# Linear attention on one core: V loaded whole and spread on chip, last two groups stored over the SP queue

## The chip, the core and the metric

The kernel runs on one core of a Trainium2 chip. A core has a matrix engine (TensorE, "PE" in the profile; its weight loads are listed apart as "PEld"), a vector engine (VectorE, "DVE"), a scalar engine (ScalarE, "ACT"), GpSimd ("POOL") and SyncE ("SP"), each with its own stream of instructions, and 16 DMA engines that move data between the large memory (HBM, "dram" in the names) and the memory on the core (SBUF). Results of the matrix engine land in a third memory, PSUM. An engine runs its instructions in order and waits on semaphores for the others. In this kernel DMAs are issued from two places: POOL's queue and SP's queue.

The metric is the device time of one execution in microseconds (us); lower is better. The kernel before took 129.44 us, the median of 8 runs (128.91 to 130.25).

## The reference

Q, K and V have 8 batches, 12 heads, 512 rows and 64 columns, in 4-byte floats. There is no softmax: a feature map replaces it, so the keys and values of a head shrink to one 64x64 matrix.

```python
Q_feat = np.maximum(0, Q) + 1
K_feat = np.maximum(0, K) + 1
KV = np.einsum('bhkd,bhkv->bhdv', K_feat, V)
K_sum = np.sum(K_feat, axis=2)
numerator = np.einsum('bhqd,bhdv->bhqv', Q_feat, KV)
denominator = np.einsum('bhqd,bhd->bhq', Q_feat, K_sum)
return numerator / (denominator[:, :, :, None] + 1e-10)
```

There is little arithmetic for each byte: three inputs and one output of 12.58 MB each have to pass between HBM and the core.

## The kernel before

The 96 heads are worked in 12 groups of 8 heads. A group's K, V and Q are each 1.05 MB in HBM. They are viewed as two blocks of 128 partitions with 16 rows of 64 columns on every partition, so one head of a block lies on 32 partitions. POOL's DMAs turn 4-byte floats into bf16 as they move them; K of group 0 alone comes over SP unchanged, as 4-byte floats.

One matmul serves four heads of a block at once, although they share the partitions, because V is laid out in blocks: the buffer `v_blk` has five column blocks; block b (0 to 3) holds V on the 32 partitions of head b and zeros elsewhere, so that each head's sum stays in its own columns. The fifth block, the edge, holds a one for each head in its first four columns and gives the key sums (`K_sum`). There are three such buffers (`NV = 3`), zeroed once at the start, partly by VectorE and partly by ScalarE; later loads overwrite only the parts that hold V. To place V in its blocks, `load_v` issues four DMAs per group, one for each 32 partitions.

The stages of a group are these.

- `k_features` and `q_features`: VectorE, two instructions each, L116; max(x + 1, 1) into the tiles `kf` and `qf`.
- `keys_values`: 32 matmuls, L141, into PSUM; ScalarE copies the result into `kva_diag`, L151 and L152.
- `transposes`: 16 transposes of Q features on the matrix engine, L160, and two copies by ScalarE into `qt`, L161.
- `output`: 32 matmuls, L173, in four parts; VectorE takes the reciprocal of the denominators, L183, and multiplies, L184, from PSUM into the output tile `o_sb`.
- `store`: one DMA of 1.05 MB from POOL, L107; for the last group two halves from SP, L110.

The order is written out by hand. In step g the kernel issues the K, Q features of g, the transposes of g-1, the output of g-2, keys_values of g, then on POOL's queue the loads of K, V and Q of g+3 (`AHEAD`) and the store of g-3 (`LAG`). K and Q have four input buffers each (`IN_BUFS`), the output has six (`OUT_BUFS`). A load waits until its buffer is free: for V that is when keys_values of three groups before is done. Every DMA of POOL also waits for the one issued eight places before it on that queue, since they share a semaphore. After the loop the last group is finished, and groups 8 to 11 are stored.

Of the kernel before, what the change touches and what calls it, by code (L numbers as in the profile page):

```python
# [8 lines left out]
FP32 = mybir.dt.float32  # L9
BF16 = mybir.dt.bfloat16  # L10
ALU = mybir.AluOpType

BANK = 512
IN_BUFS = 4
OUT_BUFS = 6
LAG = 3
AHEAD = 3


@with_exitstack  # L20
def kernel(
# [4 lines left out]
    V: bass.AP,  # L26
    out: bass.AP,
):

# [5 lines left out]
    nc = tc.nc  # L37

    B, H, S, D = Q.shape
    P = 128  # L40
    C = 8
    C2 = 2 * C
    NPAIR = B * H * S // (P * C)
    NP = 4
    NG = NPAIR // NP
# [3 lines left out]
    def view(t, c):  # L49
        return t.flatten_outer_dims().rearrange("(n p c) d -> p n c d", p=P, c=c)  # L50

    q_dram = view(Q, C2)
    k_dram = view(K, C2)
    v_dram = view(V, C2)
    o_dram = view(out, C)

    const = ctx.enter_context(tc.tile_pool(name="const", bufs=1))
    head_pool = ctx.enter_context(tc.tile_pool(name="head_pool", bufs=1))
    in_pool = ctx.enter_context(tc.tile_pool(name="in_pool", bufs=IN_BUFS))
    feat_pool = ctx.enter_context(tc.tile_pool(name="feat", bufs=2))  # L60
# [6 lines left out]

    identity = const.tile([P, P], BF16, name="identity")
    NV = 3
    v_blk = [const.tile([P, 5, 2, C2, D], BF16, name=f"v_blk{i}") for i in range(NV)]  # L70
    ones = const.tile([P, 4], BF16, name="ones")
    zero = const.tile([P, 1], FP32, name="zero")
    kva_diag = [const.tile([P, 4, 2, D1], BF16, name=f"kva_diag{i}") for i in range(NV)]

    k_in = {}
    q_in = {}
    kfs = {}
    qfs = {}
    qts = {}
    outs = {}  # L80

    def load_k(g):
        k_raw = (head_pool if g == 0 else in_pool).tile(
            [P, 2, C2, D], FP32 if g == 0 else BF16, name="k_raw"
        )
        (nc.sync if g == 0 else nc.gpsimd).dma_start(  # L86
            out=k_raw, in_=k_dram[:, g * 2 : g * 2 + 2]
        )
        k_in[g] = k_raw

    def load_v(g):
        for b in range(4):
            nc.gpsimd.dma_start(  # L93
                out=v_blk[g % NV][32 * b : 32 * b + 32, b],
                in_=v_dram[32 * b : 32 * b + 32, 2 * g : 2 * g + 2],
            )

    def load_q(g):
        q_raw = in_pool.tile([P, 2, C2, D], BF16, name="q_raw")
        nc.gpsimd.dma_start(out=q_raw, in_=q_dram[:, g * 2 : g * 2 + 2])  # L100
        q_in[g] = q_raw

    def store(g):
        o_sb = outs.pop(g)
        o_to = o_dram[:, g * NP : g * NP + NP]
        if g < NG - 1:
            nc.gpsimd.dma_start(out=o_to, in_=o_sb)  # L107
            return
        for h in range(2):
            nc.sync.dma_start(out=o_to[:, h:NP:2], in_=o_sb[:, h:NP:2])  # L110

    def edge(i):
        return v_blk[i][:, 4, :, :, 0:4].rearrange("p n c j -> p (n c) j")

    def feature(dst, src):
        nc.vector.tensor_scalar(  # L116
            out=dst, in0=src, scalar1=1.0, scalar2=1.0, op0=ALU.add, op1=ALU.max
        )

    def k_features(g):  # L120
        k_raw = k_in.pop(g)
        kf = feat_pool.tile([P, C2, 2, D], BF16, name="kf")
        for n in range(2):
            feature(kf[:, :, n], k_raw[:, n])
        kfs[g] = kf

    def q_features(g):
        q_raw = q_in.pop(g)
        qf = feat_pool.tile([P, C2, 2, D], BF16, name="qf")
        for half in range(2):  # L130
            cs = slice(half * C, half * C + C)
            feature(qf[:, cs].rearrange("p c n d -> p n c d"), q_raw[:, :, cs])
        qfs[g] = qf

    def keys_values(g):
        kf = kfs.pop(g)
        vb = v_blk[g % NV]
        kva_ps = psum_kva.tile([P, 5, D], FP32, name="kva_ps")
        for c in range(C2):
            for n in range(2):  # L140
                nc.tensor.matmul(  # L141
                    kva_ps[64 * n : 64 * n + 64],
                    lhsT=kf[:, c, n, :],
                    rhs=vb[:, :, n, c, :],
                    start=(c == 0),
                    stop=(c == C2 - 1),
                )
        kva = kva_diag[g % NV]
        for n in range(2):
            ps = slice(64 * n, 64 * n + 64)  # L150
            nc.scalar.copy(out=kva[ps, :, n, 0:D], in_=kva_ps[ps, 0:4, :])  # L151
            nc.scalar.copy(out=kva[ps, :, n, D], in_=kva_ps[ps, 4, 0:4])  # L152

    def transposes(g):
        qf = qfs.pop(g)
        qt = mid_pool.tile([P, C, P, 2], BF16, name="qt")
        for half in range(2):
            qt_ps = psum_qt.tile([P, C, P], BF16, name="qt_ps")
            for c in range(C):
                nc.tensor.transpose(qt_ps[:, c, :], qf[:, half * C + c, :, :], identity)  # L160
            nc.scalar.copy(out=qt[:, :, :, half], in_=qt_ps)  # L161
        qts[g] = qt

    def output(g):
# [26 lines left out]
                )  # L191
        outs[g] = o_sb

    with tc.manual_schedule():
        nc.gpsimd.memset(zero, 0.0)
        load_k(0)
        load_q(0)
        load_k(1)
        load_q(1)
        nc.vector.memset(ones, 0.0)  # L200
        for b in range(4):
            nc.vector.memset(ones[32 * b : 32 * b + 32, b : b + 1], 1.0)  # L202
        flat = [t.rearrange("p b n c d -> p (b n c d)").bitcast(FP32) for t in v_blk]
        width = flat[0].shape[1]
        part = width * 4 // 7
        nc.vector.memset(flat[0][:, 0:part], 0.0)  # L206
        nc.scalar.copy(  # L207
            out=flat[0][:, part:width], in_=zero.to_broadcast([P, width - part])
        )
        nc.vector.tensor_copy(out=edge(0), in_=ones[:, None, :].to_broadcast([P, 2 * C2, 4]))  # L210
        load_v(0)
        nc.vector.memset(flat[1][:, 0:part], 0.0)  # L212
        nc.scalar.copy(
            out=flat[1][:, part:width], in_=zero.to_broadcast([P, width - part])
        )
        nc.vector.tensor_copy(out=edge(1), in_=ones[:, None, :].to_broadcast([P, 2 * C2, 4]))
        make_identity(nc, identity)
        for t in kva_diag:
            nc.gpsimd.memset(t, 0.0)  # L219
        load_v(1)  # L220
        load_k(2)
        k_features(0)
        q_features(0)
        nc.vector.memset(flat[2][:, 0:part], 0.0)  # L224
        nc.scalar.copy(
            out=flat[2][:, part:width], in_=zero.to_broadcast([P, width - part])
        )
        nc.vector.tensor_copy(out=edge(2), in_=ones[:, None, :].to_broadcast([P, 2 * C2, 4]))
        load_v(2)
        load_q(2)  # L230
        for g in range(NG - 1):
            if g:
                k_features(g)
                q_features(g)
                transposes(g - 1)
            if g >= 2:
                output(g - 2)
            keys_values(g)
            if g + AHEAD < NG:
                load_k(g + AHEAD)  # L240
                load_v(g + AHEAD)
                load_q(g + AHEAD)
            if g >= LAG:
                store(g - LAG)
        last = NG - 1
        k_features(last)
        transposes(last - 1)
        output(last - 2)
        q_features(last)
        keys_values(last)  # L250
        transposes(last)
        output(last - 1)
        output(last)
        for g in range(last - LAG, NG):
            store(g)
# [30 lines left out]
```

## Time and profile before

One execution was recorded by the hardware profiler. It took 129.44 us, of which 127.7 lie between its first and its last instruction (the span).

| what | value |
|---|---|
| median of 8 runs | 129.44 us |
| the profiled execution, own time | 129.44 us |
| its span | 127.7 us |
| PE busy | 68.2 us (53%) |
| VectorE busy | 66.1 us (52%) |
| ScalarE busy | 47.2 us (37%) |
| POOL busy | 54.0 us (42%) |
| POOL's DMA queue | 29.89 MB in 13088 packets |
| SP's DMA queue | 2.10 MB in 816 packets |
| V's loads, L93 | 48 issues, mean 549 ns on POOL, median 9.4 us from issue to landing |
| K's and Q's loads from POOL | 11 and 12 issues, 712 and 731 ns, 12.0 and 11.2 us to landing |
| stores from POOL, L107 | 11 issues, 772 ns, 12.0 us to landing |

The page also divides the span into 40 slices of 3.2 us and gives for each the busy share of the engines in tenths and the bytes moved; the bytes are counted as they are written. Stretches of any length can be asked for in the same way. A group of instructions is a row: line, engine, operation, written and read names with shapes, count, busy time, mean duration in ns, and the idle time before it. The chain of waits follows the execution back from its last event to what released it, step by step.

### The profile page before, as it was taken

To read this page: it belongs to the slowest core of one execution; us is meant where nothing else is said; L and a number is where in the kernel's file an instruction comes from. 1 tells how busy PE (TensorE), PEld (TensorE's weight loads), DVE (VectorE), ACT (ScalarE), POOL (GpSimd) and SP (SyncE) were. 2 spreads that over 40 slices of the span, in tenths; PEclk is the share of its full clock that TensorE was granted. 3 is DMA by queue.
4 is the path that set the end of the run, shared out by engine and by line. 5 is a ranking of instruction groups with operands and counts; after the bars stand their busy time and mean duration, and the time that the engine had idled before them with its cause. 6 is when DMAs were issued, how large, how long until landed. Compare 5 with 4: busy or idle time off the path is not lost.

```text
span 127.7 us, 2373 instructions
## 1 busy us (share of the span) xinstructions
PE 68.2 (53%) x960; PEld 50.7 (40%) x960; DVE 66.1 (52%) x155; ACT 47.2 (37%) x76; POOL 54.0 (42%) x92
## 2 busy tenths in 40 slices
PE   0000099939569494895804932951970896853000
PEld 0000077626446373674603721741750675632000
DVE  4898702095292775929309408606524739498000
ACT  7940006950911809045540090081063045640000
POOL 6695775517345274543543462372274240201000
PEclk9999999976985999599997798699599599996555
DMA  3999999999999999999999999999999999999980
GB/s 81 336 212 209 207 207 209 209 210 210 210 205 214 207 211 211 208 341 243 209 307 278 195 264 323 208 235 351 205 220 360 213 211 375 418 415 418 404 318 1
DMA packets 13914, 32.13 MB, mean 252 GB/s; under 512 B 1360, under 2 KB 1360, under 8 KB 13904
## 3 DMA queue, kind: packets, MB, share of 16 engines
q0 software_dynamic: 13088, 29.89, 99.6%
q1 hardware_dynamic: 816, 2.10, 4.5%
q8 instruction: 7, 0.11, 0.3%
q14 instruction: 3, 0.02, 0.0%
HBM read 37.75 MB, written 12.58 MB: 394 GB/s over the span
## 4 chain that ended last, share of the span: by engine, by line
DMA 69%; DVE 11%; issue 4%; POOL 4%; PE 4%; POOLq 0%; DVEq 0%
DMA v_blk<-in_V_dram 24%; DMA out_dram<-o_sb 18%; DMA q_raw<-in_Q_dram 18%; DMA k_raw<-in_K_dram 9%; DVE o_sb L184 6%; POOL v_blk L93 4%; PE kva_ps L141 4%; DVE v_blk L206 2%; DVE recip L183 1%; DVE qf L116 1%; DVE kf L116 1%; DVE ones L202 0%; POOL q_raw L100 0%; DVE ones L200 0%; POOLq L107 0%
## 5 line engine op out<-in xcount | busy, mean ns | idle before, releaser
L141 PE MATMUL kva_ps<-v_blk,kf 128*64 128x320 bf16 x384 | 38.0, 367 | 15.7 <-DMA v_blk<-in_V_dram 15.7
L173 PE MATMUL o_ps<-kva_diag,qt 128*64 128x130 bf16 x384 | 20.6, 247 | 32.8 <-DVE o_sb L184 32.3
L93 POOL DMA_DIRECT2D v_blk<-in_V_dram x48 | 26.2, 549 | 27.8 <-DMA k_raw<-in_K_dram 12.9
L141 PEld LDWEIGHTS <-kf 128*64 128x64 bf16 x384 | 26.6, 138 | 23.7 <-DVE qf L116 15.7
L184 DVE TENSOR_TENSOR o_sb<-o_ps,recip 128x512 f32<-128x512 f32 x48 | 33.2, 691 | 1.6
L151 ACT CAST kva_diag<-kva_ps 64x256 bf16<-64x256 f32 x24 | 8.9, 371 | 64.8 <-PE kva_ps L141 64.4
L161 ACT COPY qt<-qt_ps 128x1024 bf16<-128x1024 bf16 x24 | 29.5, 1300 | 0.3
L173 PEld LDWEIGHTS <-qt 128*64 128x64 bf16 x384 | 13.7, 121 | 38.6 <-DVE o_sb L184 36.8
L116 DVE TENSOR_SCALAR qf<-q_raw 128x1024 bf16<-128x1024 bf16 x24 | 9.2, 426 | 33.1 <-DMA q_raw<-in_Q_dram 33.1
L107 POOL DMA_DIRECT2D out_dram<-o_sb x11 | 8.5, 772 | 19.9 <-DMA q_raw<-in_Q_dram 7.0
L116 DVE TENSOR_SCALAR kf<-k_raw 128x1024 bf16<-128x1024 bf16 (+1 forms) x24 | 10.9, 495 | 10.5 <-DMA k_raw<-in_K_dram 10.5
L160 PE MATMUL qt_ps<-identity,qf 128*128 128x128 bf16 x192 | 13.1, 223 | 0.0
L160 PEld LDWEIGHTS <-qf 128*128 128x128 bf16 x192 | 11.1, 100 | 3.5 <-issue 3.2
L86 POOL DMA_DIRECT2D k_raw<-in_K_dram x11 | 7.8, 712 | 8.8 <-DMA out_dram<-o_sb 5.6
L183 DVE RECIPROCAL recip<-o_ps 128x8 f32<-128x8 f32 x48 | 9.5, 198 | 3.6 <-PE o_ps L173 3.6
L100 POOL DMA_DIRECT2D q_raw<-in_Q_dram x12 | 8.8, 731 | 4.2 <-DMA v_blk<-in_V_dram 2.4
L152 ACT CAST kva_diag<-kva_ps 64x4 bf16<-64x4 f32 x24 | 4.0, 168 | 0.0
L206 DVE MEMSET v_blk<- 128x2925 f32 x1 | 2.5, 2496 | 0.7 <-DVE ones L202 0.7
L224 DVE MEMSET v_blk<- 128x2925 f32 x1 | 2.5, 2496 | 0.6 <-issue 0.6
L212 DVE MEMSET v_blk<- 128x2925 f32 x1 | 2.5, 2496 | 0.6 <-issue 0.6
L219 POOL MEMSET kva_diag<- 128x520 bf16 x3 | 2.0, 719 | 0.0
L207 ACT COPY v_blk<-zero 128x2195 f32<-128x2195 f32 x1 | 2.0, 2019 | 0.0
(15 smaller groups left out, 7.9 us busy)
## 6 DMA issues: line engine op xcount, KB each, us to landing
out_dram<-o_sb POOLq DMA_DIRECT2D x11, 1024.0 KB, 12.0
q_raw<-in_Q_dram POOLq DMA_DIRECT2D x12, 512.0 KB, 11.2
v_blk<-in_V_dram POOLq DMA_DIRECT2D x48, 128.0 KB, 9.4
k_raw<-in_K_dram POOLq DMA_DIRECT2D x11, 512.0 KB, 12.0
k_raw<-in_K_dram SPq DMA_DIRECT2D x1, 1024.0 KB, 4.9
out_dram<-o_sb SPq DMA_DIRECT2D x2, 512.0 KB, 7.5
```

The source lines that it names most:

```text
L86: (nc.sync if g == 0 else nc.gpsimd).dma_start(out=k_raw, in_=k_dram[:, g * 2 : g * 2 + 2])
L93: nc.gpsimd.dma_start(out=v_blk[g % NV][32 * b : 32 * b + 32, b], in_=v_dram[32 * b : 32 * b + 32, 2 * g : 2 * g + 2],)
L100: nc.gpsimd.dma_start(out=q_raw, in_=q_dram[:, g * 2 : g * 2 + 2])
L107: nc.gpsimd.dma_start(out=o_to, in_=o_sb)
L116: nc.vector.tensor_scalar(out=dst, in0=src, scalar1=1.0, scalar2=1.0, op0=ALU.add, op1=ALU.max)
L141: nc.tensor.matmul(kva_ps[64 * n : 64 * n + 64], lhsT=kf[:, c, n, :], rhs=vb[:, :, n, c, :], start=(c == 0), stop=(c == C2 - 1),)
L151: nc.scalar.copy(out=kva[ps, :, n, 0:D], in_=kva_ps[ps, 0:4, :])
L160: nc.tensor.transpose(qt_ps[:, c, :], qf[:, half * C + c, :, :], identity)
L161: nc.scalar.copy(out=qt[:, :, :, half], in_=qt_ps)
L173: nc.tensor.matmul(ops[c // 4][64 * j : 64 * j + 64, c // 2 % 2, (c % 2) * W : (c % 2) * W + W], lhsT=qt[:, c, 32 * b : 32 * b + 32, :], r ...
L183: nc.vector.reciprocal(out=recip, in_=cells[:, :, :, :, D:D1])
L184: nc.vector.tensor_tensor(out=o_sb[:, h:NP:2, 4 * i : 4 * i + 4].rearrange("p n (b c) d -> p b c n d", b=2), in0=cells[:, :, :, :, 0:D], i ...
```

## The change

V now comes like K and Q: one DMA puts a group's V on all 128 partitions in a plain buffer, `v_raw`. A new stage `v_blocks` copies it into its blocks, three heads' parts by VectorE and one by ScalarE, each a copy on 32 partitions. Because of that, two block buffers are enough; they lie in one tile `v_all` of nine blocks, four for even groups, four for odd ones, and the edge block between them belongs to both. `keys_values` reads five neighbouring blocks, from 0 or from 4, and its copies to `kva_diag` take the columns accordingly.

Loads are issued in pairs of groups: one DMA brings K (or V, or Q) of two groups. The first two groups and the last two are loaded one by one. Each input has two buffers of two groups. The loads of a pair are issued after keys_values of an odd group, two pairs ahead. The order on POOL at the start becomes V0, Q0, K1, V1, Q1, and K, V, Q of groups 2 and 3 after the setting up of the constants. Nine blocks are zeroed where there were three buffers of five.

The last two groups, not only the last, are stored over SP in two halves each.

```diff
+    v_all = const.tile([P, 9, 2, C2, D], BF16, name="v_all")
+    v_blk = [v_all[:, 5 * i : 5 * i + 4] for i in range(2)]
...
+    def load(s, groups, names="kvq"):
+        ms = slice(groups[0] % 2 * 2, groups[-1] % 2 * 2 + 2)
+        for x in names:
+            if (x, "buf", s) not in raw:
+                raw[x, "buf", s] = in_pool.tile([P, 4, C2, D], BF16, name=f"{x}_raw")
+            t = raw[x, "buf", s]
             nc.gpsimd.dma_start(
-                out=v_blk[g % NV][32 * b : 32 * b + 32, b],
-                in_=v_dram[32 * b : 32 * b + 32, 2 * g : 2 * g + 2],
+                out=t[:, ms], in_=drams[x][:, 2 * groups[0] : 2 * groups[-1] + 2]
             )
...
+    def load_pair(s):
+        if s < NG // 2 - 1:
+            load(s, (2 * s, 2 * s + 1))
+        else:
+            load(s, (2 * s,))
+            load(s, (2 * s + 1,))
...
-        if g < NG - 1:
+        if g < NG - 2:
             nc.gpsimd.dma_start(out=o_to, in_=o_sb)
             return
         for h in range(2):
             nc.sync.dma_start(out=o_to[:, h:NP:2], in_=o_sb[:, h:NP:2])
...
+    def v_blocks(g):
+        v_raw = raw.pop(("v", g))
+        for b in range(4):
+            ps = slice(32 * b, 32 * b + 32)
+            if b == 3:
+                nc.scalar.copy(out=v_blk[g % 2][ps, b], in_=v_raw[ps])
+            else:
+                nc.vector.tensor_copy(out=v_blk[g % 2][ps, b], in_=v_raw[ps])
...
-        vb = v_blk[g % NV]
+        sb = g % 2
+        vb = v_all[:, 4 * sb : 4 * sb + 5]
...
+    def clear(first, split, end):
+        t = v_all.rearrange("p b m c d -> p (b m c d)").bitcast(FP32)
+        w = t.shape[1] // 9
+        nc.vector.memset(t[:, first * w : split * w], 0.0)
+        nc.scalar.copy(
+            out=t[:, split * w : end * w], in_=zero.to_broadcast([P, (end - split) * w])
+        )
...
+        load_first_k()
+        load(0, (0,), "vq")
+        load(0, (1,))
...
+        load_pair(1)
+        clear(5, 7, 9)
         for g in range(NG - 1):
+            k_features(g)
+            v_blocks(g)
+            q_features(g)
             if g:
-                k_features(g)
-                q_features(g)
                 transposes(g - 1)
             if g >= 2:
                 output(g - 2)
             keys_values(g)
-            if g + AHEAD < NG:
-                load_k(g + AHEAD)
-                load_v(g + AHEAD)
-                load_q(g + AHEAD)
+            if g % 2 and g // 2 + 2 < NG // 2:
+                load_pair(g // 2 + 2)
             if g >= LAG:
                 store(g - LAG)
         last = NG - 1
         k_features(last)
+        v_blocks(last)
         transposes(last - 1)
         output(last - 2)
         q_features(last)
```

More of the change, by code (lines that the diff above doesn't have):

```diff
@@ L13 @@
 BANK = 512
-IN_BUFS = 4
+IN_BUFS = 2
 OUT_BUFS = 6
 LAG = 3
-AHEAD = 3
 @with_exitstack
@@ L69 @@
     NV = 3
-    v_blk = [const.tile([P, 5, 2, C2, D], BF16, name=f"v_blk{i}") for i in range(NV)]
+    v_all = const.tile([P, 9, 2, C2, D], BF16, name="v_all")
+    v_blk = [v_all[:, 5 * i : 5 * i + 4] for i in range(2)]
     ones = const.tile([P, 4], BF16, name="ones")
@@ L73 @@
     kva_diag = [const.tile([P, 4, 2, D1], BF16, name=f"kva_diag{i}") for i in range(NV)]
-    k_in = {}
-    q_in = {}
+    drams = dict(k=k_dram, v=v_dram, q=q_dram)
+    raw = {}
     kfs = {}
@@ L80, with own, load_first_k @@
     outs = {}
[L82 to L92, printed above, removed]
+    def own(g):
+        return slice(g % 2 * 2, g % 2 * 2 + 2)
+    def load_first_k():
+        k_raw = head_pool.tile([P, 2, C2, D], FP32, name="k_first")
+        nc.sync.dma_start(out=k_raw, in_=k_dram[:, 0:2])
+        raw["k", 0] = k_raw
+    def load(s, groups, names="kvq"):
[4 more added lines that the diff above has]
+            t = raw[x, "buf", s]
             nc.gpsimd.dma_start(
-                out=v_blk[g % NV][32 * b : 32 * b + 32, b],
-                in_=v_dram[32 * b : 32 * b + 32, 2 * g : 2 * g + 2],
-            )
[L98 to L101, printed above, removed]
+                out=t[:, ms], in_=drams[x][:, 2 * groups[0] : 2 * groups[-1] + 2]
+            )
+            for g in groups:
+                raw[x, g] = t[:, own(g)]
+    def load_pair(s):
[4 more added lines that the diff above has]
+            load(s, (2 * s + 1,))
     def store(g):
@@ L110, in store @@
             nc.sync.dma_start(out=o_to[:, h:NP:2], in_=o_sb[:, h:NP:2])
-    def edge(i):
-        return v_blk[i][:, 4, :, :, 0:4].rearrange("p n c j -> p (n c) j")
     def feature(dst, src):
@@ L120, in k_features @@
     def k_features(g):
-        k_raw = k_in.pop(g)
+        k_raw = raw.pop(("k", g))
         kf = feat_pool.tile([P, C2, 2, D], BF16, name="kf")
@@ L125, in k_features @@
         kfs[g] = kf
+    def v_blocks(g):
[6 more added lines that the diff above has]
+                nc.vector.tensor_copy(out=v_blk[g % 2][ps, b], in_=v_raw[ps])
     def q_features(g):
-        q_raw = q_in.pop(g)
+        q_raw = raw.pop(("q", g))
         qf = feat_pool.tile([P, C2, 2, D], BF16, name="qf")
@@ L150, in keys_values @@
             ps = slice(64 * n, 64 * n + 64)
-            nc.scalar.copy(out=kva[ps, :, n, 0:D], in_=kva_ps[ps, 0:4, :])
-            nc.scalar.copy(out=kva[ps, :, n, D], in_=kva_ps[ps, 4, 0:4])
+            nc.scalar.copy(out=kva[ps, :, n, 0:D], in_=kva_ps[ps, sb : sb + 4, :])
+            nc.scalar.copy(out=kva[ps, :, n, D], in_=kva_ps[ps, 4 - 4 * sb, 0:4])
     def transposes(g):
@@ L192, in output @@
         outs[g] = o_sb
+    def clear(first, split, end):
[5 more added lines that the diff above has]
+        )
     with tc.manual_schedule():
         nc.gpsimd.memset(zero, 0.0)
[L196 to L199, printed above, removed]
+        load_first_k()
+        load(0, (0,), "vq")
+        load(0, (1,))
         nc.vector.memset(ones, 0.0)
@@ L202 @@
             nc.vector.memset(ones[32 * b : 32 * b + 32, b : b + 1], 1.0)
[L203 to L216, printed above, removed]
+        clear(0, 3, 5)
+        e = v_all[:, 4, :, :, 0:4].rearrange("p n c j -> p (n c) j")
+        nc.vector.tensor_copy(out=e, in_=ones[:, None, :].to_broadcast([P, 2 * C2, 4]))
         make_identity(nc, identity)
@@ L219 @@
             nc.gpsimd.memset(t, 0.0)
[L220 to L230, printed above, removed]
+        load_pair(1)
+        clear(5, 7, 9)
         for g in range(NG - 1):
+            k_features(g)
+            v_blocks(g)
+            q_features(g)
             if g:
-                k_features(g)
-                q_features(g)
                 transposes(g - 1)
```

## The prediction

> **What bounds the kernel now.** I read the page from the slices down: first which resource is never idle, then the chain that ended last, then the stretches of the span one by one.
>
> ```profile
> span 127.7 us, 2373 instructions
> ...
> DMA  3999999999999999999999999999999999999980
> GB/s 81 336 212 209 207 207 209 209 210 210 210 205 214 207 211 211 208 341 243 209 307 278 195 264 323 208 235 351 205 220 360 213 211 375 418 415 418 404 318 1
> DMA packets 13914, 32.13 MB, mean 252 GB/s; under 512 B 1360, under 2 KB 1360, under 8 KB 13904
> ...
> HBM read 37.75 MB, written 12.58 MB: 394 GB/s over the span
> ...
> DMA 69%; DVE 11%; issue 4%; POOL 4%; PE 4%; POOLq 0%; DVEq 0%
> ```
>
> In 37 of 40 slices the DMA engines are 90% busy or more; no compute engine passes 53% of the span. The rate row looks uneven, but it counts what is written: a load turns 4-byte values into 2-byte ones, so 209 GB/s of loads is 418 GB/s read, the same as the 418 of the stores at the end. At 418 GB/s, 37.75 + 12.58 = 50.33 MB take 120.4 us of the 127.7. So the DMA engines are the bound, and the change can only matter through the bytes' rate, the head, the tail, or a new hole in the DMA work.
>
> The stretches, with the last two columns the busy share of the DMA engines and GB/s:
>
> ```profile
> 5.00:11.00 6.00, 0.00 (x0) 0.00 (x0) 5.60 (x6) 2.89 (x2) 5.69 (x11) 1.00 1.12 212
> 12.00:17.00 5.00, 1.31 (x10) 1.05 (x12) 3.25 (x6) 0.00 (x0) 3.21 (x6) 1.00 1.12 206
> 17.00:50.00 33.00, 25.03 (x344) 18.73 (x340) 15.48 (x41) 15.78 (x30) 16.42 (x28) 0.90 1.12 210
> 107.00:117.00 10.00, 6.85 (x120) 4.99 (x120) 8.00 (x21) 3.57 (x7) 1.51 (x2) 0.96 1.02 417
> 119.00:123.00 4.00, 0.00 (x0) 0.00 (x0) 0.00 (x0) 0.00 (x0) 0.00 (x0) 0.50 1.02 397
> ...
> 124.00:125.00 1.00, 0.00 (x0) 0.00 (x0) 0.00 (x0) 0.00 (x0) 0.00 (x0) 0.50 0.12 45
> 125.00:127.70 2.70, 0.00 (x0) 0.00 (x0) 0.00 (x0) 0.00 (x0) 0.00 (x0) 0.50 0.00 0
> ```
>
> In program order the POOL queue carries Q0, K1, Q1 (one DMA each) and then V0 and V1 (four DMAs each). The first row is the former, the second the latter: the same bytes in four pieces run at 206 instead of 212 GB/s. Data end at about 124.7; then 3.0 us without a transfer close the program. Two lines from the chain of waits show what the end hangs on:
>
> ```profile
> 100.66 10.49 DMA out_dram<-o_sb
> ...
> 117.05 0.69 DVE o_sb L184
> ```
>
> VectorE finishes at 117.7, seven microseconds before the last byte: compute has slack, because stores are still queued.
>
> **What the Trainium skill says.** "DMA: Bandwidth & Descriptors", section "Anatomy of one DMA — SWDGE (gpsimd) path", calls the semaphore write that ends a DMA nearly free on trn2, about one cycle. The two rows above disagree, or something else costs the small DMAs: per 0.52 MB, 2.545 against 2.473 us, so 72 ns for three more DMAs, 24 ns each. I follow the trace. The same page's "Issuing engines are not separate DMA queues" says that SP's and POOL's DMAs share the 16 engines: moving stores to SP opens no bandwidth (397 GB/s at 119 to 123, where both queues ran, agrees). "SBUF — State Buffer", section "Who interferes with whom", says that a VectorE copy in a two-port mode and GpSimd work exclude each other; the copy at L216 (980 ns, its twins 138 and 129) fits.
>
> ```profile
> L213 ACT COPY v_blk<-zero 128x2195 f32<-128x2195 f32 x1 | 2.0, 2014 | 0.0
> ...
> L216 DVE COPY v_blk<-ones 128x128 bf16<-128x128 bf16 x1 | 1.0, 980 | 0.0
> ...
> L210 DVE COPY v_blk<-ones 128x128 bf16<-128x128 bf16 x1 | 0.1, 138 | 0.0
> L228 DVE COPY v_blk<-ones 128x128 bf16<-128x128 bf16 x1 | 0.1, 129 | 0.0
> ```
>
> **The change, part by part.**
>
> Fewer DMAs. POOL loads before: 11 K, 12 Q, 48 V = 71. After: groups 0, 1, 10 and 11 alone, 2 to 9 in pairs, 7 K + 8 V + 8 Q = 23. At 24 ns, 48 fewer save 48 × 0.024 = 1.15 us on a path busy throughout. Bytes and their pieces of 4 KB read and 2 KB written are unchanged. Bounds: nothing, if the semaphore write is free as the page says; 1.9 us at 39 ns, which 2 GB/s of error in either row allows.
>
> Stores of group 10 over SP in halves. The mixed tail ran at 397, POOL's stores alone at 417: 5% on 1.05 MB, 2.5 us, costs 0.13 us. Bounds 0 and 0.3 (if the loss spreads over two groups).
>
> Head. K0 still goes first over SP and POOL's first issue still stands at 1.3 us. V0 and Q0 now follow with no wait on zeroing; before, the queue held Q0, K1, Q1 until 12 us, so the wait of V0's issue (4.75 us) cost nothing and saves nothing. The clearing falls from 15 blocks to 9; all of it ran under DMA. 0.
>
> Longer look-ahead. Loads of a pair are issued up to four groups ahead, after the odd group's work, and stores stand behind them on POOL's queue. Is there a hole? One group's K, V or Q, or one store, is 2.5 us of DMA. Head to pair 1 is 12 such units: work until 1.8 + 30 = 32 us. Pair 2 is issued from about 14 to 21 us (after VectorE's K, V, Q work of group 1 and ScalarE's V copy behind the first keys_values): 11 us early. Pair 3 waits for group 3's conversion, about 44 us at the latest, with work until 47 plus its own K already queued to 52. Later pairs stand behind stores and earlier loads with more. POOL also waits for its DMA eight issues back; eight of the new ones hold at least two groups. Nothing runs dry, 0; the store of group 0 lands later (about 65 us), but its buffer is not wanted before group 6's output, some 20 us on.
>
> V copies. VectorE gets three copies of 2048 bf16 per group, ScalarE one. No row of before has this form. The nearest, the bf16 conversions of 1024 (L116), take 420 ns and come 0.34 apart; doubled that is 0.7 us. "VectorE: DVE Perf Modes", "The perf-mode tier table", prices the copy at 693 ns, and at 1227 ns for the fp32 form, one mode lower. I take 0.70, with 0.6 and 1.23 as ends: 2.1 us per group, 25 us in all, on an engine idle for 61. ScalarE: "ScalarE: Activation LUTs", "What ACT_TABLE_LOAD costs", gives 186 + 0.833 × 2048 = 1892 ns (its formula gives 2014 for L213, as measured); 22.7 us on an engine busy 47. ScalarE's copy stands behind the previous group's kva copies and ahead of the qt copies, so keys_values now waits 1.1 + 1.9 us after the one before; PE's transposes and output matmuls, paced by VectorE at 0.84 × 4 = 3.36 us a group, fill that time. Cost 0 while covered by DMA.
>
> Does the cover hold at the end? Up to Q of groups 8 and 9, 30 loads and 2 stores pass: 1.8 + 32 × 2.5 = 82 us, say 83. From there VectorE owes Q8 (0.76), K, V, Q of three groups (3 × 3.6 = 10.9) and six outputs (6 × 3.36 = 20.2): 32 us, end 115, with PE waits before the last outputs 117. Before it was 117.7. The last stores are issued when DMA still has over 6 us of work. What is late next is only the queue itself.
>
> Sum: −1.15 + 0.13 = −1.0 us. Span 126.7, data end 123.7. The profiled execution took 129.44, 1.7 more than its span, and 129.44 is also the median; so 128.4.
>
> **The rivals.**
> A, the forecast: fewer DMAs give about 1 us, 128.4 (own range 127.6 to 129.0). For it: the two rates and a DMA row without a hole.
> B, no change: the 6 GB/s come from the place of the V blocks or chance, or a late SP half takes the gain. For it: the page's "nearly free", and 17 to 50, with V in it, at 210. Against: then 206 is hard to explain. 129.4.
> C, slower: VectorE becomes the bound, through its copies alone, if each takes 1.23 us (a lower mode on 32 partitions, or waits on POOL's descriptor writing). A group then costs 1.52 + 3.69 + 3.36 = 8.6 us. From Q2's landing at 33: 0.76 + 9 × 5.2 + 12 × 3.36 = 88, end 121.5 to 123; SP's halves then go through an emptied queue, data end near 126, span 129.4, time 131.1. It decides from about 1.1 us a copy. Against: the conversions show the fast mode on the same types, with medians near the minimum (420 against 406 ns).
> D, it doesn't do what it says: V's single DMA moves no faster and POOL runs out of issues. Excluded as far as I can see by the counts above; its time is B's.
>
> **Numbers.** A 0.56, B and D 0.22, C 0.22. Under 0.5% (0.65 us) a measurement of this kernel can hardly tell from no change. Faster takes most of A; same takes B and A's edge; slower is C. The range 127.5 to 131.2 takes in A, B and most of C.
>
> **What would show it.** Right: loads at 211 to 213 GB/s in V's stretches too; about 608 packets under 512 B (38 DMAs × 16) in place of 1360; the DMA row without a gap; data ending near 123.7; VectorE's last write at 116 to 118. The V copies' rows: 0.7 and 1.9 us. Wrong: DMA slices under 9 between 10 and 120 us; VectorE writing output past 120; a load rate unchanged at 209, which would make semaphore writes free; copies over 1.1 us.

## The result and the profile after

The kernel after took 127.44 us, the median of 11 runs (126.88 to 128.46), against 129.36 for the kernel before in the same comparison: a ratio of 0.9848 with a 95% interval of 0.9825 to 0.9871. By the medians it is 1.9 us faster, where 1.0 was forecast. The profiled execution took 127.08 us with a span of 125.3; before they were 129.44 and 127.7. It is one of the faster ones, so the two traces differ by more (2.35 us in the span) than the medians do.

The page of the kernel after, in the lines that were shown of the kernel before:

```profile
span 125.3 us, 2337 instructions
...
DMA  3999999999999999999999999999999999999993
GB/s 95 330 211 210 212 200 208 212 213 211 212 210 216 210 212 211 214 211 215 232 415 309 200 212 212 211 341 400 227 211 210 213 258 419 417 418 411 401 401 128
DMA packets 13419, 32.13 MB, mean 256 GB/s; under 512 B 608, under 2 KB 608, under 8 KB 13408
...
DMA 70%; DVE 13%; issue 6%; POOL 4%; PE 3%; POOLq 0%; DVEq 0%
```

The DMA row has no gap, as before; the packets under 512 B fell from 1360 to 608, as forecast. The last slice tells something new: it is partly busy now, where before it stood at 0. The span ends sooner after the last byte. The stretches of the kernel after (the last two columns are the busy share of the DMA engines and GB/s) show the same:

```profile
5.00:11.00 6.00, 0.30 (x4) 0.21 (x6) 5.88 (x7) 2.62 (x2) 4.37 (x9) 1.00 1.12 211
12.00:17.00 5.00, 4.62 (x40) 3.12 (x36) 2.22 (x5) 1.68 (x5) 0.74 (x1) 1.00 1.12 210
17.00:50.00 33.00, 15.02 (x224) 11.78 (x224) 19.21 (x42) 17.42 (x23) 5.61 (x7) 0.79 1.12 211
...
117.00:121.00 4.00, 0.84 (x16) 0.51 (x16) 2.72 (x7) 0.00 (x0) 0.00 (x0) 0.68 1.03 400
...
123.00:124.00 1.00, 0.00 (x0) 0.00 (x0) 0.00 (x0) 0.00 (x0) 0.00 (x0) 0.50 0.38 145
124.00:125.30 1.30, 0.00 (x0) 0.00 (x0) 0.00 (x0) 0.00 (x0) 0.00 (x0) 0.50 0.00 0
```

The packet records of the two traces give the last byte exactly: 124.69 us before, 124.08 after. So of the 2.35 us by which the span fell, 0.61 came from the transfers and 1.74 from what follows them: 2.98 us before, 1.23 after. What closes the program shows in the waits of SP's queue. First the kernel before (total us, times, longest us):

```profile
SPq L281 <- DMA out_dram<-o_sb: 6.6, 3, 5.2
SPq L281 <- PEq L281: 2.4, 2, 1.9
```

and the kernel after:

```profile
SPq L284 <- DMA out_dram<-o_sb: 3.6, 3, 1.2
SPq L284 <- PEq L284: 0.7, 2, 0.5
```

In each the first row is the wait for the stores to land, the second the meeting of all engines that follows, in two waits. Before, the longer of the two took 1.9 us and the other 0.5; after, the longer is 0.5 and the other 0.2. The total fell from 2.4 to 0.7: these are the 1.7 us. The view names PE's queue, but PE's last matmul had ended at 116.8 us in the trace before: the instruction records show POOL in a closing drain, an instruction that counts as no work and so stands in no row. Before, it began at 114.65 us and lasted until 126.89, while SP was ready at 125.2. After, it ended at 120.74, ahead of SP's 124.5.

### The profile page after: what moved, and what is told of

It reads as the page before. It is cut to its first block, busy times and chain, and to the rows that moved or that the text cites. A ratio compares the mean times of both kernels' runs of the same rounds, so it can differ in the third digit from the quotient of the medians.

```text
span 125.3 us, 2337 instructions
## 1 busy us (share of the span) xinstructions
PE 66.9 (53%) x960; PEld 49.9 (40%) x960; DVE 88.3 (70%) x188; ACT 68.0 (54%) x87; POOL 27.8 (22%) x43
## 3 DMA queue, kind: packets, MB, share of 16 engines
q1 hardware_dynamic: 1360, 3.15, 6.6%
## 4 chain that ended last, share of the span: by engine, by line
DMA 70%; DVE 13%; issue 6%; POOL 4%; PE 3%; POOLq 0%; DVEq 0%
DMA out_dram<-o_sb 37%; DMA q_raw<-in_Q_dram 24%; DMA v_raw<-in_V_dram 9%; DVE o_sb L200 8%; DVE v_all L140 2%; POOL v_raw L99 2%; PE kva_ps L157 2%; DVE recip L199 1%; PE qt_ps L176 1%; POOL out_dram L116 1%; POOL q_raw L99 1%; PE o_ps L189 1%; DVE qf L122 1%; DVE kf L122 1%; POOL k_raw L99 0%
## 5 line engine op out<-in xcount | busy, mean ns | idle before, releaser
L157 PE MATMUL kva_ps<-v_all,kf 128*64 128x320 bf16 x384 | 37.3, 362 | 12.2 <-DVE v_all L140 10.7
L189 PE MATMUL o_ps<-kva_diag,qt 128*64 128x130 bf16 x384 | 19.5, 238 | 39.5 <-DVE o_sb L200 38.9
L140 DVE COPY v_all<-v_raw 32x2048 bf16<-32x2048 bf16 x36 | 26.6, 738 | 10.5 <-DMA v_raw<-in_V_dram 10.1
L138 ACT COPY v_all<-v_raw 32x2048 bf16<-32x2048 bf16 x12 | 22.7, 1894 | 12.2 <-DMA v_raw<-in_V_dram 12.0
L99 POOL DMA_DIRECT2D k_raw<-in_K_dram x7 | 5.3, 755 | 37.4 <-DVE kf L122 37.4
L122 DVE TENSOR_SCALAR kf<-k_raw 128x1024 bf16<-128x1024 bf16 x22 | 8.7, 439 | 6.0 <-DMA k_raw<-in_K_dram 6.0
L99 POOL DMA_DIRECT2D v_raw<-in_V_dram x8 | 6.0, 752 | 19.7 <-ACT v_all L138 11.5
L99 POOL DMA_DIRECT2D q_raw<-in_Q_dram x8 | 5.9, 741 | 4.3 <-DMA q_raw<-in_Q_dram 4.3
L213 DVE MEMSET v_all<- 128x3072 f32 (+1 forms) x2 | 4.4, 2192 | 1.1 <-DVE ones L225 0.7
L214 ACT COPY v_all<-zero 128x2048 f32<-128x2048 f32 x2 | 3.7, 1894 | 0.0
```

The source lines that it names most:

```text
L99: nc.gpsimd.dma_start(out=t[:, ms], in_=drams[x][:, 2 * groups[0] : 2 * groups[-1] + 2])
L122: nc.vector.tensor_scalar(out=dst, in0=src, scalar1=1.0, scalar2=1.0, op0=ALU.add, op1=ALU.max)
L138: nc.scalar.copy(out=v_blk[g % 2][ps, b], in_=v_raw[ps])
L140: nc.vector.tensor_copy(out=v_blk[g % 2][ps, b], in_=v_raw[ps])
L157: nc.tensor.matmul(kva_ps[64 * n : 64 * n + 64], lhsT=kf[:, c, n, :], rhs=vb[:, :, n, c, :], start=(c == 0), stop=(c == C2 - 1),)
L189: nc.tensor.matmul(ops[c // 4][64 * j : 64 * j + 64, c // 2 % 2, (c % 2) * W : (c % 2) * W + W], lhsT=qt[:, c, 32 * b : 32 * b + 32, :], r ...
```

## The experiments

Two theories stood against each other. T: fewer DMAs gave some 0.7 us, and 1.7 came because POOL's queue now ends before SP's, so POOL's closing drain no longer holds up the end. R1: all 2 us are the price of 48 DMAs, 42 ns each. R2: what cost was V's place on 32 partitions, not the count of DMAs. The first four runs share the runs of before (129.54 us).

**The store change alone.** The kernel before, with one line changed:

```diff
-        if g < NG - 1:
+        if g < NG - 2:
             nc.gpsimd.dma_start(out=o_to, in_=o_sb)
```

> The kernel before, with the store of group 10 also over SP in halves and nothing else of the change. Theory T (the change gained in two parts: about 0.7 us from fewer DMAs and 1.7 us because POOL's queue now falls silent before SP's, so that POOL's closing drain no longer ends the program): 127.8 us, with POOL's closing drain over before SP's last half lands and the program ending about 1.2 us after the last byte. Rival R1 (all of the gain is the price of a DMA, 2.0 us over 48 DMAs, 42 ns each): 129.5 us, no gain.

Measured: 127.73 us, a ratio of 0.9864 (0.9825 to 0.9903). 81 DMAs are still on POOL, yet 1.8 us are gone, so R1 falls. Its last byte came at 124.58 us, 0.11 earlier than before; the drain ended at 124.66, just before SP was ready at 125.07, and the meeting was short again:

```profile
SPq L281 <- PEq L281: 0.7, 2, 0.5
```

**The load change alone.** The kernel after, with that line changed back:

```diff
-        if g < NG - 2:
+        if g < NG - 1:
```

> The kernel after, with only the last group's store over SP, so that group 10 goes over POOL as before: the load side of the change alone. T: 128.8 us, data ending near 124.0 and the program some 3 us after it. R1: 127.4 us, the whole gain kept.

Measured: 127.50 us, 0.9838 (0.9798 to 0.9879). T was wrong here: group 10 goes over POOL again, and the closing gain stays. POOL's last byte was at 121.76 us and the drain ended at 123.61, only 1.85 us later; before it had been 3.82. So the drain itself is shorter with fewer DMAs. Either half of the change hides the drain alone, which is why their gains don't add. The transfers gave less here than in the full change, with the last byte at 124.33: the store of group 10, issued at 116.8 us, had waited for all four parts of its output, and the DMA engines ran short at 117 us.

```profile
117.00:119.00 2.00, 1.01 (x16) 0.60 (x16) 1.93 (x6) 0.00 (x0) 0.56 (x1) 0.84 0.80 315
```

The busy share is 0.80, where the kernel after had 1.03 from 117 to 121. With the halves of group 10 over SP the last byte comes 0.25 us earlier in these two traces; in the medians, 127.50 and 127.44, no difference shows.

**More DMAs, cut by blocks.** The kernel after, its loads cut into blocks of 128 partitions:

```diff
-            nc.gpsimd.dma_start(
-                out=t[:, ms], in_=drams[x][:, 2 * groups[0] : 2 * groups[-1] + 2]
-            )
+            for n in range(2 * len(groups)):
+                nc.gpsimd.dma_start(
+                    out=t[:, ms.start + n], in_=drams[x][:, 2 * groups[0] + n]
+                )
```

> The kernel after, each load cut into its blocks of 128 partitions: 70 loads from POOL in place of 23, same pieces in each packet. T (22 ns a DMA): 127.4 + 47 x 0.022 = 128.4 us. R1 (42 ns): 129.4 us. Rival R2 (what cost V before was its place on 32 partitions, not the count): 127.4 us.

Measured: 127.96 us, 0.9876 (0.9835 to 0.9918). The last byte came at 124.98 us, 0.90 later than in the kernel after, for 47 more DMAs: 19 ns each on the DMA engines. The median rose by only 0.52, which is 11 ns each (the trace of the kernel after was of one of its faster executions). That is T's mechanism at a smaller price. R1's 42 ns is out. R2's zero misses the place of the last byte, but the intervals of the two medians lie over each other; a count over more traces, told with the prediction below, decides against it.

**More DMAs, cut by partitions.** The same loads, in pieces of 32 partitions as V had before:

```diff
+            for b in range(4):
+                ps = slice(32 * b, 32 * b + 32)
+                nc.gpsimd.dma_start(
+                    out=t[ps, ms],
+                    in_=drams[x][ps, 2 * groups[0] : 2 * groups[-1] + 2],
+                )
```

> The kernel after, each load cut into four of 32 partitions: 92 loads from POOL in place of 23. T (22 ns a DMA): 127.4 + 69 x 0.022 = 128.9 us. R1 (42 ns): 130.3 us. R2 (a load on 32 partitions runs 3% slower, now for all 90 us of loads): about 130 us, and unlike T far above the version cut by blocks.

Measured: 132.74 us, 1.0246 (1.0196 to 1.0297), slower than every theory had it. A hole in the DMA work explains part. The stretches of this run:

```profile
5.00:11.00 6.00, 0.42 (x4) 0.50 (x6) 4.88 (x6) 2.62 (x2) 4.57 (x9) 1.00 1.12 207
...
17.00:18.00 1.00, 0.00 (x0) 0.11 (x1) 0.62 (x1) 0.98 (x1) 1.00 (x2) 1.00 0.81 146
18.00:19.00 1.00, 0.04 (x2) 0.04 (x3) 0.07 (x1) 0.98 (x2) 1.00 (x3) 1.00 0.03 6
19.00:20.00 1.00, 1.00 (x16) 1.00 (x17) 0.73 (x2) 1.00 (x1) 1.00 (x3) 1.00 0.77 39
20.00:21.00 1.00, 1.00 (x19) 1.00 (x16) 0.00 (x0) 1.00 (x2) 1.00 (x3) 1.00 1.01 143
21.00:50.00 29.00, 12.14 (x166) 8.65 (x161) 14.51 (x33) 10.94 (x15) 14.24 (x25) 0.71 1.12 209
```

POOL is busy all through the hole (1.00 in the fifth column): it needs about 0.55 us for every small DMA and got to the loads of groups 2 and 3 only at 18.05 us. The four microseconds average 84 GB/s, not 209: 2.4 us are lost. Of the 5.5 us by which the last byte came later, some 3 remain; 69 DMAs at 19 ns are 1.3 of them. R2's 3% on all loads does not show after the hole (209 against the kernel after's 211). By the packet records this run was 3.7 us behind the kernel after at 90 us, which the hole and the price of the DMAs explain. Another 0.9 us went between 90 and 105 us, where POOL issued DMAs almost without a pause, and 0.9 after 115 us. What took those is open.

**The closing drain.** Now there was a better theory, D: the drain ends a fixed time plus a price per DMA after POOL's last byte. Over the runs so far:

```
run, DMAs on POOL, POOL's last byte (us), end of the drain (us), later by (us)
kernel after         33    118.93    120.74    1.81
load change alone    34    121.76    123.61    1.85
cut by blocks        80    120.95    124.69    3.74
store change alone   81    120.88    124.66    3.78
kernel before        82    123.07    126.89    3.82
cut by partitions   102    125.20    129.86    4.66
```

These come from the instruction and packet records of each trace. The straight line through them is 0.45 us + 0.041 us per DMA. To see it without anything in front of it, the next two runs send the very last half store over POOL, so that the drain comes last; the second one also cuts the loads by blocks. They share the runs of before (129.47 us) with two runs told below, the one with whole stores and the one in which ScalarE copies two heads.

```diff
         for h in range(2):
-            nc.sync.dma_start(out=o_to[:, h:NP:2], in_=o_sb[:, h:NP:2])
+            queue = nc.gpsimd if (g, h) == (NG - 1, 1) else nc.sync
+            queue.dma_start(out=o_to[:, h:NP:2], in_=o_sb[:, h:NP:2])
```

> The kernel after, with the very last half store over POOL in place of SP, so that POOL's queue ends last. Theory D (POOL's closing drain ends 0.45 us + 0.041 us for each DMA that POOL issued after its last byte, the line through the runs so far: 1.81 us at 33 DMAs, 3.8 at 82): with 34 DMAs and data to about 124.1 the drain ends near 125.9, 1.85 us after POOL's last byte, and the span at 126.7, so 128.7 us. Rival F (the drain takes 3.8 us when POOL ends late, whatever the count): 130.6 us. Rival N (the queue that ends last doesn't matter): 127.4 us.

> The same with each load cut into its blocks of 128 partitions, 81 DMAs on POOL. D: data to about 125.0, drain 3.8 us after, span 129.5, so 131.3 us, 2.6 above the run before this one, of which 1.9 are the drain's and about 0.7 the DMA engines'. F: only about 0.7 above it. N: 127.9 us.

Measured: 128.49 us, 0.9932 (0.9907 to 0.9957), and 131.01 us, 1.0117 (1.0068 to 1.0167). D foretold 128.7 and 131.3; F and N are out. The drains ended 1.79 and 3.73 us after POOL's last byte, for the same bytes in 34 and in 81 DMAs. The meeting of the engines, first in the run with 34,

```profile
SPq L285 <- PEq L285: 1.7, 2, 1.3
```

and then in the run with 81:

```profile
SPq L286 <- PEq L286: 3.7, 2, 3.2
```

**Whole stores over SP.** The kernel after, with

```diff
-        for h in range(2):
-            nc.sync.dma_start(out=o_to[:, h:NP:2], in_=o_sb[:, h:NP:2])
+        nc.sync.dma_start(out=o_to, in_=o_sb)
```

> The kernel after, with the last two groups stored over SP in one DMA each, not in halves. If the 5% slower tail is a matter of the halves' 2 KB packets (84 ns each against 159 for 4 KB), whole stores bring back 4 KB packets and up to 0.3 us: 127.1 us. If instead the later start of the last store (1.7 us) leaves the DMA engines idle at the end, or the packets stay at 2 KB: 127.5 to 128.5 us.

Measured: 126.99 us, 0.9814 (0.9774 to 0.9853). The time is near the first forecast, but not for its reason: the packets stayed at 2 KB (1024 of them, 85 ns each), for which 127.5 to 128.5 us was expected. The last byte, at 123.97 us, is only 0.11 before that of the kernel after. In a later comparison (129.41 us for before), which it shares with three runs told below (one V copy, doubled copies, and the two ideas together), the kernel after was run again:

> The kernel after, once more, beside the others on one chip: 127.4 us, ratio to before 0.985. Where the version with whole stores stood at 126.99, a ratio of 0.9814, the difference of 0.4 us is real if this run gives 0.985 again, and not if it gives 0.982.

Measured: 127.32 us, 0.9831 (0.9804 to 0.9857). It lies between the two values named, and the intervals lie over each other: no difference is shown.

**Does VectorE's later end cost anything?** In the kernel after VectorE writes its last output at 119.83 us, 2.1 later than before. Four runs moved that point. Here VectorE copies one head of V, not three:

```diff
-            else:
+            elif b == 0:
                 nc.vector.tensor_copy(out=v_blk[g % 2][ps, b], in_=v_raw[ps])
```

> The kernel after, with VectorE copying one head of V per group and not three; heads 1 and 2 of every block are left out, so the sums of half the heads are zero. If the copies as they stand already cost time at the end, VectorE's last write falls from 119.8 to about 117 and up to 0.5 us comes back: 127.0 us. If queued stores cover all of it: 127.4 us.

Measured: 127.40 us, 0.9843 (0.9814 to 0.9871), with VectorE's last write at 116.9. Nothing came back: stores still queued cover VectorE as it stands. The other way, each of its V copies twice:

```diff
-                nc.vector.tensor_copy(out=v_blk[g % 2][ps, b], in_=v_raw[ps])
+                for _ in range(2):
+                    nc.vector.tensor_copy(out=v_blk[g % 2][ps, b], in_=v_raw[ps])
```

> The kernel after, with every one of VectorE's V copies made twice (6 per group, 0.68 us each, the same result). Theory T (VectorE's copies are covered only until about 1.1 us per copy; VectorE's last write at 119.8 us stands near the edge): a group costs VectorE 1.5 + 4.1 + 3.4 = 9.0 us, VectorE becomes the bound, its last write comes near 126, the last stores follow an emptied queue: 132 to 134 us. Rival (VectorE has idle time enough, 70% busy): 127.4 us.

Measured: 136.65 us, 1.0555 (1.052 to 1.0589). In the same comparison the kernel after took 127.32 us. The direction is T's, the size is 3 us over it, for VectorE's last write came at 131.1, not 126; VectorE was busy for only 20.9 of the 25 us from 100 to 125, and I had counted it busy throughout. The busy row of the DMA engines in this run shows the emptied queue at the end:

```profile
DMA  4999999999999999999999999999999997408384
```

So the copies were free at 0.7 us a head, and at twice that they cost 9.3 us; the edge lies between. Moving one head's copy from VectorE to ScalarE, so that each has two, brings another wait:

```diff
-            if b == 3:
+            if b >= 2:
```

> The kernel after, with two heads of V copied by VectorE and two by ScalarE. VectorE's last write came at 119.8 us, 2.1 later than before; if that lateness costs anything (the DMA engines partly idle after 117), VectorE ends 2 us earlier and up to 0.5 us comes back: 127.0 us. If stores still queued cover it: 127.4 us. If ScalarE's two copies (3.8 us ahead of its qt copies) become the chain: over 128 us.

Measured: 128.40 us, 0.9900 (0.9874 to 0.9927). In its waits, PE now stands behind ScalarE's V copies:

```profile
PE kva_ps L157 <- ACT v_all L138: 25.2, 10, 12.1
...
DVE recip L199 <- PE o_ps L189: 12.4, 8, 4.7
```

The first row is 1.5 us in all in the kernel after. The second is VectorE's wait for PE's output; VectorE's last write slips to 122.6 us. The same for the last two groups only, with whole stores, was tried as the best of both (`if b == 3 or (b == 2 and g >= NG - 2)`):

> The version with whole stores over SP, and in the last two groups two heads of V copied by ScalarE and two by VectorE. VectorE's last write 1.4 us earlier, if ScalarE's extra 1.9 us stays beside VectorE's work: 126.7 us. If ScalarE's copy ahead of keys_values becomes the chain, as with two heads in all groups: over 127.4 us. No cover lost or won: 127.0 us.

Measured: 128.03 us, 0.9860 (0.9822 to 0.9898), the runs compared spread from 126.98 to 128.14. No gain is shown. After 95 us PE waited 1.8 us in total for ScalarE's V copies and VectorE 5.3 for PE's output (2.6 in the kernel after), and VectorE's last write came at 121.1. No version was found that is shown to be faster than the kernel after.

## Why the prediction was right or wrong

The direction and the bound were right: the DMA engines stayed full, no hole appeared, and the change was faster. The time was not: 127.44 us lies below the forecast's own range and just below the lower end of the whole one, 127.5.

*The close.* The step that failed is "then 3.0 us without a transfer close the program". I read it as a constant and carried it through the sum (data end 123.7, span 126.7); it measured 1.23 us. Of the 3.0 us, 1.7 were a wait: POOL's drain, which ends 0.45 us + 0.041 per DMA after POOL's last byte, came to an end 1.7 us after SP was ready. The change shortened it (33 DMAs for 82) and started it earlier (POOL's last byte at 118.93 for 123.07), and either was enough to hide it. The row of SP's waits, 1.9 us in the meeting of the engines, was there to be read in the profile before; the prediction used only the DMA stretches of the tail. The other error pulled the opposite way: the transfers gained 0.4 us less than the sum said, and this hid a part of the 1.7.

*Fewer DMAs, 1.15 us.* The mechanism was right, the size was too large. At 112 us, with all loads in, the kernel after had moved 0.32 MB more, by the packet records, which at 418 GB/s is 0.77 us: 16 ns for each of the 48 loads saved. The same count over other traces: the nine with 23 loads from POOL stood 0.22 to 0.36 MB ahead of the kernel before, the store change alone (71 loads) 0.06 ahead, and the two with loads cut by blocks (70) 0.04 to 0.05 behind. So it goes with the count of the loads, 14 to 18 ns each. V on 32 partitions, as the kernel before and the store change alone have it, did no worse than loads on 128 partitions in nearly the same number, so R2 is out. The two head stretches ran at 211 and 210 GB/s in the kernel after, where 211 to 213 was expected. My 24 ns came from two stretches of five and six microseconds, 206 and 212, where one GB/s weighs 4 ns. The bound of nothing came from the Trainium skill, which calls the semaphore write essentially free, about one cycle ("DMA: Bandwidth & Descriptors", "Anatomy of one DMA — SWDGE (gpsimd) path"). On DMA engines that are busy throughout it was not free here: these small writes stand in the packet records with a median of 22 ns on POOL's queue.

*Stores of group 10 over SP, 0.13 us.* The price of the packets was right: 512 packets of 2 KB at 84.6 ns in place of 256 of 4 KB at 161.4 make 2.0 us of engine time, 0.12 us over 16 engines. At the last byte no such cost was seen: it came 0.11 us earlier than before with the store change alone, and 0.25 us later than in the kernel after without it. The second has a reason that the prediction left out, the DMA engines running short when the store waits for its whole output. The 0.11 us is no more than the 0.06 MB by which these two traces, with the same loads, already differed at 112 us (0.15 us at 418 GB/s). The sum of both terms for the last byte was 1.0 us; it was 0.61.

*Head and look-ahead, 0.* Right; the store of group 0, said to land at about 65 us, landed at 65.0, 20 us before group 6's output was written.

*V copies.* The rows of the kernel after:

```profile
L140 DVE COPY v_all<-v_raw 32x2048 bf16<-32x2048 bf16 x36 | 26.6, 738 | 10.5 <-DMA v_raw<-in_V_dram 10.1
...
L138 ACT COPY v_all<-v_raw 32x2048 bf16<-32x2048 bf16 x12 | 22.7, 1894 | 12.2 <-DMA v_raw<-in_V_dram 12.0
```

VectorE's 738 ns, with a median of 684, stand beside 693 in the Trainium skill, "VectorE: DVE Perf Modes", "The perf-mode tier table"; ScalarE's 1894 beside the estimate of 1892 from its "ScalarE: Activation LUTs", "What ACT_TABLE_LOAD costs". I had VectorE's last write at 117, or 116 to 118; it was 119.83. Of the 2.8 us, 1.25 are that Q of groups 8 and 9 was taken up at 84.25 and not 83, and some 0.7 that the copies took 2.35 us a group at the end, not 2.1; the rest I have not traced. The cover still held, as the run with fewer copies shows.

*The rivals.* B, no change, is excluded by the time, and its free DMAs by the cut loads. C, VectorE as the bound, is real but not at 0.7 us a copy: doubled copies cost 9.3 us. D did not occur.

## What to carry to other kernels

When a profile ends with microseconds in which nothing moves, ask which engine arrived last at the final meeting; here it was the queue that had issued 82 DMAs, and either issuing fewer or letting another queue finish last took 1.7 us away. Two edits that hide the same wait must be priced together: their gains do not add. Where DMA is the bound, as here, work put on the other engines is free only until its last product meets the end of the transfer queue; measure how far off that is by doubling and by removing it.

## What the runs showed of the hardware

POOL's closing drain lasted 0.45 us + 0.041 us for every DMA that POOL had issued, counted from its last byte, over 33 to 102 DMAs (1.8 to 2.1 us in all runs with 33). The same bytes in 34 and 81 DMAs gave 1.79 and 3.73 us, and with 33 it was 1.82 us where the drain began at 108.0 us (one V copy) and 1.81 where it began at 110.9 (the kernel after). A DMA from POOL cost the DMA engines 14 to 19 ns beyond its bytes by the packet records (11 by the medians of the run cut by blocks and the kernel after). Where the drain ended the program, 47 more DMAs cost 2.52 us, 54 ns each. POOL itself needed about 0.55 us to issue a load on 32 partitions: with all loads cut so, it left the DMA engines idle for 2.4 us at the head.
